# A two-layer decoder trunk on one core: hi and lo activations in one matmul of the feed-forward up-projection

## Chip, cores, metric

One core of one Trainium2 chip runs the whole program in one launch. The metric is device time in microseconds (us), the median of the timed runs. Five engines work in parallel, each through its own queue in program order: PE (TensorE, matmul), DVE (VectorE), ACT (ScalarE), POOL (GpSimd) and SP (SyncE, which here issues the loads).

## What is computed

x is 256 tokens of 1024 channels. Layer 0 has a sparse-attention mixer, layer 1 a state-space (SSD) mixer; each mixer is followed by a gated feed-forward with a causal convolution of width 3 along the tokens:

```python
def conv_ffn(h, w_up, conv_w, conv_b, w_down):
    u = causal_dwconv(h @ w_up, conv_w, conv_b)
    val, gate = u[..., :FFN_HIDDEN], u[..., FFN_HIDDEN:]
    return (jax.nn.silu(gate) * val) @ w_down
```

FFN_HIDDEN is 2816. The mixers take no part in the change.

## The kernel before, in words

**Products in three parts.** Every fp32 operand is split into a high part (a copy to fp32r by ACT) and a low part (source minus high, by DVE; `split`, L55 to L58). A product is then three matmuls: high by high, high by low, low by high (`mm3`, L166).

**Weights.** `Weights` (L71) loads a weight tile in halves of 128x1024 on SP's queue into `raw` (5 buffers), ACT casts the half to `whi` (L56), DVE makes `wlo` (L57), each from 5 buffers. A cast can start once PE is done with the buffer that it takes and the load has landed; the load can start once the `raw` buffer has been read.

**Feed-forward** (`ffn`, L536). The hidden channels are cut in 22 pairs p: 128 value channels (m=0) and the 128 gate channels that belong to them (m=1), each over all 256 tokens. Pairs 0 and 1 go through `proj_halves` (L183), while the second half of the tokens is still being normalised. Pairs 2 to 21 go through `pair` (L205): `proj_t` makes, for each m, 8 x 3 matmuls of 256 columns into one PSUM bank `pu` (two such banks are in turn). From `pu`, ACT makes the first tap of the convolution with the bias (`tap0`, L528), DVE the two other taps (`taps`, L534), ACT the gate's SiLU (L561), DVE the gate product (L562), and ACT and DVE split the result into the two parts of `hm`. The down-projection `down` takes `hm` of pair p-5 (LAG is 5): 12 matmuls of 512 columns into four banks `acc`. The last pairs' down-projections (5 in layer 0, 4 in layer 1; T0, T1) are left to the end, the first tokens' ahead of the second's; their weights have buffers of their own.

**What sets the order.** Each engine runs its queue as written. A conversion of weights stands in the queues of ACT and DVE where the recording layer put it, between the steps of the pairs, and whatever waits there holds what stands behind it. Before the feed-forward of layer 0 stands the attention; behind it the SSD mixer, whose first weights are loaded in the feed-forward's tail. Behind the feed-forward of layer 1 only the last normalisation and the store follow.

Of the kernel before, what the change touches and what calls it, by code (L numbers as in the profile page):

```python
# [7 lines left out]
F32 = mybir.dt.float32  # L8
F32R = mybir.dt.float32r
# [3 lines left out]
OP = mybir.AluOpType  # L13
AX = mybir.AxisListType

S, D = 256, 1024
KT = D // 128
FH = 2816
NP = FH // 128
# [14 lines left out]
def trunk(ctx, tc, x, gains, consts, masks, params, nsa_in, nsa_vw, cmp_w1, nsa_out,  # L34
          ssd_in, ssd_dt, ssd_out, ffn_up, ffn_down, out):
    nc = tc.nc
    cp = ctx.enter_context(tc.tile_pool(name="cp", bufs=1))
# [5 lines left out]
    def pa(shape, name):  # L43
        return pp.tile(shape, F32, name=name, tag="k" if name in ("pu", "pk", "pv", "po") else "t", bufs=2)

    def ps_(shape, name):
        return pp.tile(shape, F32, name=name, tag="s", bufs=4)
# [7 lines left out]
    def split(hi, lo, src, copy=nc.scalar.copy, eng=nc.vector):  # L55
        r = copy(hi, src)  # L56
        eng.tensor_tensor(lo, src, hi.bitcast(F32), op=OP.subtract)  # L57
        return r.ins  # L58

    def mm(*a, **k):  # L60
        last_mm[0] = nc.tensor.matmul(*a, **k)  # L61
        return last_mm[0]
# [30 lines left out]
    weights = Weights  # L93
# [33 lines left out]
        return rstd_of(ss[:, 0:1], ss[:, 1:2], 1)  # L127

    def new_xt():
        return (cp.tile([128, 2, KT, 128], F32R, name="xhi"), cp.tile([128, 2, KT, 128], F32R, name="xlo"))  # L130

    def after_ins(ins):
        return tc.issue_after(ins) if ins is not None else nullcontext()
# [37 lines left out]
    def proj_t(o, w, xt, c0, n=128):  # L171
        for k in range(KT):
            r = mm3(o, *w(k, slice(c0, c0 + n)), xt[0][:, :, k, :], xt[1][:, :, k, :], k == 0, k == KT - 1)
        return r.ins
# [8 lines left out]
    def proj_halves(ws, xt, pool, extra=None):  # L183
        marks = []
        u = [[pool.tile([128, 256], F32, name="ut", bufs=2 * len(ws)) for i in range(2)] for w in ws]
        for n, w in enumerate(ws):
            proj_half(w, xt, 0, u[n][0], marks)
        if extra:
            extra(0)
        pend(*marks[-FB:][:2])  # L190
        if extra:
            extra(1)
        for n in range(len(ws) + 1):
            if n < len(ws):
                proj_half(ws[n], xt, 1, u[n][1], marks)
            if n == 0:
                continue
            n -= 1
            ps = ps_([128, 2, S], "pu")
            for i in range(2):  # L200
                for m in range(2):
                    tr(ps[:, m, 128 * i:128 * i + 128], u[n][i][:, 128 * m:128 * m + 128], ident)
            yield ps

    def pair(w, xt, wide=False, order=[None]):  # L205
        ps = (ps_ if wide else pa)([128, 2, S], "pu")
        for m in range(2):
            order[0] = proj_t(ps[:, m, :], w, xt, 128 * m)
        return ps

    def out_mm(acc, i, jobs, first, last):
        marks = []
        ts = slice(128 * i, 128 * i + 128)
        for n, (a, ka, w, kw) in enumerate(jobs):
            for c in range(2):
                cs = slice(512 * c, 512 * c + 512)
                marks.append(mm3(acc[c], a[0][:, ka, ts], a[1][:, ka, ts], *w(kw, cs), first and n == 0,
                                 last and n == len(jobs) - 1).ins)
        return marks
# [307 lines left out]
    def tap0(c, ps, base, nt):  # L527
        nc.scalar.activation(c, ps, AF.Identity, bias=pr[:, base + nt:base + nt + 1],  # L528
                             scale=pr[:, base + nt - 1:base + nt])

    def taps(c, ps, base, nt):
        for s in range(1, nt):
            wv = pr[:, base + nt - 1 - s:base + nt - s]
            nc.vector.scalar_tensor_tensor(c[:, s:], ps[:, :S - s], wv, c[:, s:], op0=OP.mult, op1=OP.add)  # L534

    def ffn(l, fp, xt, after):  # L536
        lag, tail, nf = LAG, (T0, T1)[l], (N0, N1)[l]
        ex = max(tail, 2 * nf - 4)
        hs, wd = {}, {}
        first = proj_halves([weights(ffn_up[NP * l + p], KT, 256, *((fp, ex) if p >= 2 else ())) for p in range(nf)], xt, fp) if nf else None  # L540

        accs = []

        def down(ps, i):
            if not accs:
                accs.extend([ps_([128, 512], "acc") for c in range(2)] for i in range(2))
            return out_mm(accs[i], i, [(hs[p], 0, wd[p // 2], p % 2) for p in ps], ps[0] == 0, ps[-1] == NP - 1)

        for p in range(NP + lag):
            if p < NP:  # L550
                if p < nf:
                    ps = next(first)
                else:
                    ps = pair(weights(ffn_up[NP * l + p], KT, 256), xt)
                cc = fp.tile([128, 2, S], F32, name="cc", bufs=3)
                for m in (1, 0):
                    tap0(cc[:, m, :], ps[:, m, :], P_FC + 176 * l + 8 * p + 4 * m, 3)
                for m in (1, 0):
                    taps(cc[:, m, :], ps[:, m, :], P_FC + 176 * l + 8 * p + 4 * m, 3)
                    if m:  # L560
                        silu[0] = nc.scalar.activation(cc[:, 1, :], cc[:, 1, :], AF.Silu).ins  # L561
                nc.vector.tensor_tensor(cc[:, 0, :], cc[:, 0, :], cc[:, 1, :], op=OP.mult)  # L562
                hm = fp.tile([128, 2, 1, S], F32R, name="hm", bufs=tail + lag + 1)
                hs[p] = [hm[:, 0], hm[:, 1]]
                split(hm[:, 0, 0], hm[:, 1, 0], cc[:, 0, :])
            q = p - lag
            if q >= 0 and q % 2 == 0:
                late = q >= NP - tail
                wd[q // 2] = weights(ffn_down[(NP // 2) * l + q // 2], 2, D, *((fp, ex) if late else ()))
            if 0 <= q < NP - tail:  # L570
                for i in range(2):
                    down([q], i)
        marks = [down(range(NP - tail, NP), i) for i in range(2)][1]
        after(0, accs[0], marks[-FA:][:2])
        after(1, accs[1])


    def ssd(zp, yp, xt):
# [19 lines left out]
        def bc_unit(u, ps=None):  # L598
            if ps is None:
                ps = pair(weights(ssd_in[16 + u], KT, 256), xt, True)  # L600
            for m in range(2):
                t = 2 * u + m
                conv_tile(ps[:, m, :], 16 + t, bT[:, t, :] if t < 4 else cT[:, t - 4, :])
# [232 lines left out]


    xt = new_xt()
    gain0 = load_gain(0)
    scaled, *marks0 = prenorm(0, gain0, xt)  # L840
# [48 lines left out]
    for n, layer in enumerate((nsa, lambda *a: ffn(0, *a), ssd, lambda *a: ffn(1, *a))):  # L889
        nxt = new_xt() if n < 3 else None  # L890
        with tc.tile_pool(name=f"layer{n}", bufs=1) as pool:
            if n == 2:
                with tc.tile_pool(name="scan", bufs=1) as yp:
                    state = ssd(pool, yp, xt)
                with tc.tile_pool(name="ssd_out", bufs=1) as op_:
                    ssd_out_phase(op_, state, boundary(nxt))
            else:
                layer(pool, xt, boundary(nxt))
        xt = nxt
# [99 lines left out]
```

## Time and profile before

| | |
|---|---|
| runs | 740.83, 739.77, 740.40 us; median 740.4 |
| the profiled execution | 737.78 us, of which span 736.0 us |
| granted TensorE clock, mean | 0.993 |
| PE busy | 713.1 us (97%) |
| DVE busy | 567.2 us (77%) |
| ACT busy | 466.7 us (63%) |
| POOL busy | 75.8 us (10%) |

How to read it: the span is the profiled execution from its first to its last instruction; busy time is summed over the whole program, in which stages of different limits follow one another. A matmul's record is longer than its share of the engine, since matmuls overlap; what one costs in a stream is the stream's length over its count.

### The profile page before, as it was taken

Reading aid. Unit: us, or ns where it says so; the run is one execution under the profiler, and the core shown is the slowest. Engines: PE = TensorE matmul, PEld = TensorE weight load, DVE = VectorE, ACT = ScalarE, POOL = GpSimd, SP = SyncE. Lnnn points to the kernel's source line nnn. Section 1 sums busy time; section 2 is a strip of 40 time slices with the busy share of each in tenths; the row PEclk is TensorE's granted clock in tenths of the full one; section 3 lists DMA queues with packets and bytes.
Section 4 is the critical chain, followed back from the end, with each engine's and each line's share of the span. In section 5 each row is a group of like instructions: output and inputs, shape, how many; then the busy total and the mean of one; then the engine's idle time right before and its main releaser. Section 6 shows DMA issues by size and latency. Waiting matters only on the chain.

```text
span 736.0 us, 13745 instructions
## 1 busy us (share of the span) xinstructions
PE 713.1 (97%) x5252; PEld 658.0 (89%) x5252; DVE 567.2 (77%) x994; ACT 466.7 (63%) x879; POOL 75.8 (10%) x113
## 2 busy tenths in 40 slices
PE   7998999999999999999999999999989999999996
PEld 4998986779999999997999999998779999999995
DVE  4688898667867777688698878898888877767783
ACT  5577997447656555566776687765647655555551
POOL 2321442120000000001000000133120000000000
PEclk8999999999999999999999999999999999999998
DMA  8865431425655665564445574144655656555531
GB/s 313 297 220 181 140 119 59 142 79 185 199 197 173 193 202 182 195 218 154 139 166 172 181 232 133 58 139 148 200 172 172 200 175 200 197 185 189 181 106 57
DMA packets 35426, 126.07 MB, mean 171 GB/s; under 512 B 4065, under 2 KB 4385, under 8 KB 35361
## 3 DMA queue, kind: packets, MB, share of 16 engines
q1 hardware_dynamic: 35360, 125.20, 51.9%
q8 instruction: 41, 0.67, 0.4%
q14 instruction: 25, 0.20, 0.1%
HBM read 124.14 MB, written 1.05 MB: 170 GB/s over the span
## 4 chain that ended last, share of the span: by engine, by line
PE 77%; DVE 8%; ACT 7%; DMA 4%; issue 2%; POOL 1%; SPq 0%; DVEq 0%; POOLq 0%; ACTq 0%
PE pu L61 45%; PE acc L61 18%; PE pv L61 5%; DVE wlo L57 4%; ACT P L391 2%; PE pt L65 2%; ACT whi L56 2%; PE po L61 2%; ACT junk L126 1%; DMA raw<-in_nsa_in 1%; PE py L61 1%; DMA raw<-in_ffn_down 1%; DMA raw<-in_cmp_w 1%; DVE gw L799 1%; DMA raw<-in_ssd_out 1%
## 5 line engine op out<-in xcount | busy, mean ns | idle before, releaser
L57 DVE TENSOR_TENSOR wlo<-raw,whi 128x1024 fp32r<-128x1024 f32 (+1 forms) x219 | 270.5, 1240 | 79.9 <-ACT whi L56 79.2
L56 ACT CAST whi<-raw 128x1024 fp32r<-128x1024 f32 x223 | 230.8, 1045 | 111.0 <-PE pu L61 56.6
L61 PE MATMUL pu<-xhi,whi 128*128 128x256 f32 x1056 | 296.0, 281 | 1.5 <-DVE graw L288 1.5
L61 PE MATMUL pu<-xhi,wlo 128*128 128x256 f32 x1056 | 295.0, 280 | 1.5 <-DVE wlo L57 1.5
L61 PE MATMUL pu<-xlo,whi 128*128 128x256 f32 x1056 | 294.6, 279 | 0.0
L61 PEld LDWEIGHTS pu<-xhi,whi 128*128 128x128 f32 x1056 | 198.5, 188 | 3.4 <-ACT kd L358 1.6
L61 PEld LDWEIGHTS pu<-xhi,wlo 128*128 128x128 f32 x1056 | 198.4, 188 | 2.2 <-DVE wlo L57 2.1
L61 PEld LDWEIGHTS pu<-xlo,whi 128*128 128x128 f32 x1056 | 198.5, 188 | 1.2
L534 DVE SCALAR_TENSOR_TENSOR cc<-pu,pr,cc 128x255 f32<-128x255 f32 (+2 forms) x248 | 111.3, 477 | 6.7 <-ACT cc L528 3.6
L61 PE MATMUL acc<-whi,hm 128*128 128x512 f32 x352 | 114.6, 390 | 0.1
L61 PEld LDWEIGHTS acc<-whi,hm 128*128 128x128 f32 x352 | 66.1, 188 | 13.8 <-ACT hm L56 0.6
L61 PE MATMUL acc<-wlo,hm 128*128 128x512 f32 x176 | 68.9, 392 | 0.0
L528 ACT ACTIVATE cc<-pu,pr 128x256 f32<-128x256 f32 x112 | 57.8, 559 | 8.9 <-PE pu L61 8.8
L117 POOL TENSOR_SCALAR ms<-ss 128x1 f32<-128x1 f32 x16 | 7.9, 491 | 416.3 <-ACT junk L126 416.3
L56 ACT CAST hm<-cc 128x256 fp32r<-128x256 f32 x44 | 17.8, 404 | 44.9 <-DVE cc L562 44.9
L61 PE MATMUL acc<-whi,gw 128*128 128x512 f32 x128 | 41.3, 397 | 0.0
L61 PEld LDWEIGHTS acc<-wlo,hm 128*128 128x128 f32 x176 | 33.0, 188 | 5.6
L61 PE MATMUL pv<-whi,xhi 128*128 128x256 f32 (+1 forms) x128 | 36.8, 300 | 0.9 <-ACT xhi L56 0.4
L61 PE MATMUL pv<-whi,xlo 128*128 128x256 f32 (+1 forms) x128 | 35.5, 294 | 1.0 <-DVE xlo L57 0.9
L61 PE MATMUL pv<-wlo,xhi 128*128 128x256 f32 (+1 forms) x128 | 35.2, 285 | 0.2 <-DVE wlo L57 0.2
L391 ACT ACTIVATE P<-P,mx 128x128 f32<-128x128 f32 (+1 forms) x64 | 28.3, 447 | 2.9 <-DVE mx L389 2.9
L57 DVE TENSOR_TENSOR hm<-cc,hm 128x256 fp32r<-128x256 f32 x44 | 18.6, 424 | 14.6 <-ACT hm L56 14.6
(205 smaller groups left out, 862.7 us busy)
## 6 DMA issues: line engine op xcount, KB each, us to landing
raw<-in_ffn_up SPq DMA_DIRECT2D x88, 512.0 KB, 4.3
raw<-in_ffn_down SPq DMA_DIRECT2D x44, 512.0 KB, 4.6
raw<-in_ssd_in SPq DMA_DIRECT2D x40, 512.0 KB, 4.4
raw<-in_nsa_in SPq DMA_DIRECT2D x18, 512.0 KB, 5.1
raw<-in_ssd_out SPq DMA_DIRECT2D x16, 512.0 KB, 4.3
gain<-in_gains SPq DMA_DIRECT2D x8, 512.0 KB, 4.7
raw<-in_cmp_w SPq DMA_DIRECT2D x8, 512.0 KB, 6.3
raw<-in_nsa_out SPq DMA_DIRECT2D x8, 512.0 KB, 3.7
```

The source lines that it names most:

```text
L56: r = copy(hi, src)
L57: eng.tensor_tensor(lo, src, hi.bitcast(F32), op=OP.subtract)
L61: last_mm[0] = nc.tensor.matmul(*a, **k)
L65: last_mm[0] = nc.tensor.transpose(*a)
L117: nc.gpsimd.tensor_scalar(ms, a, b, EPS, op0=OP.mult if isinstance(b, float) else OP.add, op1=OP.add)
L126: nc.scalar.activation(junk, src[c], AF.Square, scale=1.0 / 32, accum_out=ss[:, c:c + 1])
L391: nc.scalar.activation(p, p, AF.Exp, scale=-1.0, bias=mx[:, qt, b:b + 1], accum_out=sums[:, qt, hh, b + 1:b + 2])
L528: nc.scalar.activation(c, ps, AF.Identity, bias=pr[:, base + nt:base + nt + 1], scale=pr[:, base + nt - 1:base + nt])
L534: nc.vector.scalar_tensor_tensor(c[:, s:], ps[:, :S - s], wv, c[:, s:], op0=OP.mult, op1=OP.add)
L799: nc.vector.scalar_tensor_tensor(gw[1][:, t, :], gg[:, t, :], nw, gw[0][:, t, :].bitcast(F32), op0=OP.mult, op1=OP.subtract)
```

## The change

Pairs 2 to 19 of each layer (36 in all) are made by a new `pair_wide`; pairs 0, 1, 20 and 21 stay as they are. The two parts of the activations now lie in one tile, so that one matmul of 512 columns multiplies a high weight by both parts; a second of 256 columns multiplies the low weight by the high part. A pair thus has 32 matmuls in place of 48, over the same 12288 columns. The gate half comes first and has a PSUM bank `pt`, the value half a bank `pv`. The two halves of a bank are then added into an SBUF tile `up`: ACT copies one, DVE adds the other; `tap0` and `taps` read `up`. The gate product of these pairs goes to POOL.

```diff
@@ -127,7 +127,8 @@
     def new_xt():
-        return (cp.tile([128, 2, KT, 128], F32R, name="xhi"), cp.tile([128, 2, KT, 128], F32R, name="xlo"))
+        both = cp.tile([128, 2, 2, KT, 128], F32R, name="xt")
+        return both[:, 0], both[:, 1], both.rearrange("p a b k t -> p (a b) k t")
@@ -207,6 +208,20 @@
+    def pair_wide(w, xt, dst):
+        for m in (1, 0):
+            ps = pa([128, 2, S], ("pv", "pt")[m])
+            cols = slice(128 * m, 128 * m + 128)
+            for k in range(KT):
+                hi, lo = w(k, cols)
+                if k:
+                    mm(ps[:, 0, :], lo, xt[0][:, :, k, :], start=False, stop=False)
+                mm(ps.rearrange("p a b -> p (a b)"), hi, xt[2][:, :, k, :], start=(k == 0), stop=(k == KT - 1))
+                if not k:
+                    mm(ps[:, 0, :], lo, xt[0][:, :, k, :], start=False, stop=False)
+            nc.scalar.copy(dst[:, m, :], ps[:, 1, :])
+            nc.vector.tensor_tensor(dst[:, m, :], ps[:, 0, :], dst[:, m, :], op=OP.add)
@@ -550,8 +565,11 @@
                 if p < nf:
                     ps = next(first)
+                elif p >= NP - 2:
+                    ps = pair(weights(ffn_up[NP * l + p], KT, 256), xt)
                 else:
-                    ps = pair(weights(ffn_up[NP * l + p], KT, 256), xt)
+                    ps = fp.tile([128, 2, S], F32, name="up", bufs=2)
+                    pair_wide(weights(ffn_up[NP * l + p], KT, 256), xt, ps)
@@ -559,7 +577,7 @@
-                nc.vector.tensor_tensor(cc[:, 0, :], cc[:, 0, :], cc[:, 1, :], op=OP.mult)
+                (nc.gpsimd if nf <= p < NP - 2 else nc.vector).tensor_tensor(cc[:, 0, :], cc[:, 0, :], cc[:, 1, :], op=OP.mult)
```

DVE's queue in the middle of layer 0's feed-forward, before the change: one pair from behind its predecessor's last step to its own (`cc` is the pair's convolution, `wlo` a converted weight half, `hm` the split result).

```order
L57 TENSOR_TENSOR wlo_3206<-raw_3203,whi_3205 128x1024
L57 TENSOR_TENSOR wlo_3212<-raw_3209,whi_3211 128x1024
L534 SCALAR_TENSOR_TENSOR cc_3106<-pu_3057,pr_126,cc_3106 128x255
L534 SCALAR_TENSOR_TENSOR cc_3106<-pu_3057,pr_126,cc_3106 128x254
L534 SCALAR_TENSOR_TENSOR cc_3106<-pu_3057,pr_126,cc_3106 128x255
L534 SCALAR_TENSOR_TENSOR cc_3106<-pu_3057,pr_126,cc_3106 128x254
L57 TENSOR_TENSOR wlo_3230<-raw_3227,whi_3229 128x1024
L562 TENSOR_TENSOR cc_3106<-cc_3106 128x256
L57 TENSOR_TENSOR hm_3115<-cc_3106,hm_3115 128x256
```

Two conversions stand ahead of the pair's taps, the third behind them, then the gate product and the low part of `hm`. The same stretch of DVE's queue after the change:

```order
L224 TENSOR_TENSOR up_2942<-pt_2955,up_2942 128x256
L549 SCALAR_TENSOR_TENSOR cc_2993<-up_2942,pr_125,cc_2993 128x255
L549 SCALAR_TENSOR_TENSOR cc_2993<-up_2942,pr_125,cc_2993 128x254
L57 TENSOR_TENSOR wlo_3083<-raw_3080,whi_3082 128x1024
L224 TENSOR_TENSOR up_2942<-pv_2974,up_2942 128x256
L57 TENSOR_TENSOR wlo_3089<-raw_3086,whi_3088 128x1024
L549 SCALAR_TENSOR_TENSOR cc_2993<-up_2942,pr_125,cc_2993 128x255
L549 SCALAR_TENSOR_TENSOR cc_2993<-up_2942,pr_125,cc_2993 128x254
L57 TENSOR_TENSOR wlo_3108<-raw_3105,whi_3107 128x1024
L57 TENSOR_TENSOR hm_3002<-cc_2993,hm_3002 128x256
```

Two adds are new, the conversions lie between the gate's and the value's steps, and the gate product is gone to POOL's queue, where it stands alone; the third conversion is right ahead of the low part of `hm`, which needs that product.

ACT's queue at the same place, before the change (`x2`: two in a row):

```order
L56 CAST whi_3023<-raw_3021 128x1024
L56 CAST whi_3029<-raw_3027 128x1024
L528 ACTIVATE cc_2924<-pu_2875,pr_126 128x256 x2
L56 CAST whi_3047<-raw_3045 128x1024
L561 ACTIVATE cc_2924<-cc_2924 128x256
L56 CAST hm_2933<-cc_2924 128x256
```

The casts of the weights run ahead of the steps that wait for DVE. After the change:

```order
L223 COPY up_2942<-pt_2955 128x256
L543 ACTIVATE cc_2993<-up_2942,pr_125 128x256
L56 CAST whi_3082<-raw_3080 128x1024
L579 ACTIVATE cc_2993<-cc_2993 128x256
L223 COPY up_2942<-pv_2974 128x256
L56 CAST whi_3088<-raw_3086 128x1024
L543 ACTIVATE cc_2993<-up_2942,pr_125 128x256
L56 CAST whi_3107<-raw_3105 128x1024
L56 CAST hm_3002<-cc_2993 128x256
```

Two copies are new, and the second and third cast now stand behind the gate's SiLU (L579), which waits for DVE's taps.

## Rows read from the trace of the kernel before

**Rows 1.** Chain that ended last: start, length (us), work; both feed-forwards.

```profile
173.56 22.17 PE pu L61 x190
195.73 2.75 PE acc L61 x12
198.48 5.60 PE pu L61 x48
...
312.51 1.06 ACT whi L56
...
327.56 3.87 DMA raw<-in_ssd_in
...
337.60 7.81 PE acc L61 x33
...
713.36 15.68 PE acc L61 x69
```

**Rows 2.** Windows: PE, PEld, DVE, ACT, POOL busy us (instructions), clock, DMA share, GB/s.

```profile
220.00:300.00 80.00, 80.00 (x573) 75.08 (x572) 59.10 (x88) 46.74 (x69) 0.00 (x0) 1.00 0.58 188
...
558.00:580.00 22.00, 22.00 (x189) 21.95 (x188) 20.49 (x37) 15.71 (x28) 0.00 (x0) 1.00 0.68 214
```

**Rows 3.** Groups by line and form, ACT, 160 to 340 us.

```profile
L56 ACT CAST whi<-raw 128x1024 fp32r<-128x1024 f32 x65 | 67.9, 1050 | 40.9 <-PE pu L61 20.3 <-PE acc L61 13.4 <-DMA raw<-in_ssd_in 3.0
L528 ACT ACTIVATE cc<-pu,pr 128x256 f32<-128x256 f32 x44 | 22.4, 559 | 0.0
L561 ACT ACTIVATE cc<-cc 128x256 f32<-128x256 f32 x22 | 9.1, 414 | 3.4 <-DVE cc L534 3.4
L56 ACT CAST hm<-cc 128x256 fp32r<-128x256 f32 x22 | 8.9, 404 | 21.4 <-DVE cc L562 21.4
L181 ACT COPY ut<-pv 128x256 f32<-128x256 f32 x4 | 1.5, 368 | 2.7 <-PE pv L61 2.7
L126 ACT ACTIVATE junk<-h 128x512 bf16<-128x512 f32 x2 | 1.3, 632 | 1.9 <-DVE h L164 1.9
L126 ACT ACTIVATE junk<-acc 128x512 bf16<-128x512 f32 x2 | 1.2, 597 | 1.1 <-PE acc L61 1.1
```

**Rows 4.** Groups by line and form, DVE, 160 to 340 us.

```profile
L57 DVE TENSOR_TENSOR wlo<-raw,whi 128x1024 fp32r<-128x1024 f32 x66 | 80.5, 1222 | 29.5 <-ACT whi L56 29.5
L534 DVE SCALAR_TENSOR_TENSOR cc<-pu,pr,cc 128x254 f32<-128x254 f32 x44 | 21.1, 481 | 1.4
L57 DVE TENSOR_TENSOR hm<-cc,hm 128x256 fp32r<-128x256 f32 x22 | 9.3, 424 | 7.1 <-ACT hm L56 7.1
L562 DVE TENSOR_TENSOR cc<-cc 128x256 f32<-128x256 f32 x22 | 9.2, 419 | 0.2
```

**Rows 5.** Timeline of DVE in layer 0's feed-forward: start us, length us.

```profile
255.16 1.23 DVE L57 TENSOR_TENSOR wlo<-raw,whi 128x1024 fp32r<-128x1024 f32 x1 [0.18 <-ACT whi L56]
256.31 1.90 DVE L534 SCALAR_TENSOR_TENSOR cc<-pu,pr,cc 128x255 f32<-128x255 f32 x4
258.12 1.22 DVE L57 TENSOR_TENSOR wlo<-raw,whi 128x1024 fp32r<-128x1024 f32 x1
...
262.11 1.23 DVE L57 TENSOR_TENSOR wlo<-raw,whi 128x1024 fp32r<-128x1024 f32 x1 [1.53 <-ACT whi L56]
```

**Rows 6.** Timeline of PE, the matmul that first reads that conversion.

```profile
266.73 0.28 PE L61 MATMUL pu<-xhi,wlo 128*128 128x256 f32 x1
```

**Rows 7.** Timeline of POOL in the SSD mixer's end.

```profile
490.76 1.60 POOL L803 TENSOR_TENSOR sq<-sq 128x256 f32<-128x256 f32 x1
...
495.81 0.81 POOL L803 TENSOR_TENSOR sq<-sq 128x256 f32<-128x256 f32 x1
```

**Rows 8.** Timeline of DVE at the same places.

```profile
490.22 1.54 DVE L57 TENSOR_TENSOR wlo<-raw,whi 128x1024 fp32r<-128x1024 f32 x1 [1.21 <-ACT whi L56]
...
495.94 1.76 DVE L57 TENSOR_TENSOR wlo<-raw,whi 128x1024 fp32r<-128x1024 f32 x1
```

**Rows 9.** Timeline of ACT in layer 0's feed-forward: casts of pair 18 and of pair 21.

```profile
309.79 0.41 ACT L56 CAST hm<-cc 128x256 fp32r<-128x256 f32 x1 [1.40 <-DVE cc L562]
...
337.14 0.41 ACT L56 CAST hm<-cc 128x256 fp32r<-128x256 f32 x1 [1.35 <-DVE cc L562]
```

**Rows 10.** Timeline of DVE, the last step of layer 1's pair 21.

```profile
717.37 0.43 DVE L57 TENSOR_TENSOR hm<-cc,hm 128x256 fp32r<-128x256 f32 x1 [0.47 <-ACT hm L56]
```

## The prediction

> **What bounds the kernel now.** I first read the chain that ended last [rows 1]. In both feed-forwards it lies on PE: 22.17 us for the opening pairs 2 to 5, which have no down-projection beside them yet, then for each pair 5.60 us of up-projection and 2.75 us of down-projection, a period of 8.35 us. In layer 0's tail, from 312.5 us, it leaves PE and runs through weight casts, conversions and loads until PE can go on at 337.6 us; in layer 1's tail it stays on PE. Second, the windows [rows 2]: from 220 to 300 us PE is busy 80.00 of 80 us at the full granted clock, DVE 59.1, ACT 46.7, POOL not at all. So in the steady part only PE's time counts, and the other engines have cover: DVE 2.2 us per period of 8.35. In the opening (558 to 580 us) the cover is thin: DVE is busy 20.49 of 22 us. The question is therefore what PE saves, and whether DVE, ACT and POOL, which now pass each pair between them more often, still fit in PE's period.
>
> **What PE saves.** A matmul of 256 columns takes 5.60/48 = 116.7 ns of the stream, one of 512 takes 2.75/12 = 229.1 ns [rows 1]. The change replaces two of the first by one of the second: 2 x 116.7 - 229.1 = 4.3 ns. With 16 merged per pair that is 0.07 us per pair, so PE's period becomes 8.28 us; 36 pairs give 2.5 us, half of it in each layer. If a merged matmul beside a short one does not cost as the down-projection's does, the gain lies between nothing (512 columns as dear as two times 256, 233.3 ns) and twice this (225 ns). I take the down-projection's 229.1, since it is the same operand type and width on the same engine. The Trainium skill, page "TensorE: Matmul & The Clock Gate", section "Back-to-back issue gap", gives N/2.4 + 2.5 ns for a lone matmul of N columns; by it a merge saves the 2.5 ns alone, 576 merges 1.4 us in place of my 2.5, and the trace's two cadences are both above the formula's 109.2 and 215.8 ns.
>
> **What the other engines get.** Per pair:
> - ACT: two copies of 128x256 out of PSUM, 0.37 us each [rows 3]; the first taps read SBUF in place of PSUM. The Square of 512 elements is 0.035 us longer from SBUF than from PSUM [rows 3], so I take 0.59 for the tap's 0.56. ACT goes from 4.9 us per period to 5.7, under the period.
> - DVE: two adds of 128x256, 0.42 each [rows 4]; the taps keep their 0.48, to be checked; the gate product, 0.42, goes. DVE's work grows from 6.2 to 6.6 us: by itself hidden.
> - POOL: one product of 128x256 of two SBUF operands. The nearest rows are the SSD mixer's: 0.81 us where nothing held it, 1.60 us where a DVE conversion ran when it started [rows 7]. That conversion ran from 490.22 to 491.76 and the POOL product ended at 492.36, 0.60 us behind it [rows 7, 8]. The other way round, a conversion of 1.22 us that met a POOL product took 1.76 us, ending 1.08 us behind it (495.94 to 497.70, product until 496.62). So these two do not run side by side; each waits out the other.
>
> **The loop.** More counts than the sum: DVE's queue now has the third conversion right ahead of the low part of hm, which needs POOL's product, and POOL can only end 0.60 us behind that conversion. I follow one pair when DVE's side is late and PE's results lie ready. Start at an hm cast. Handoffs are 0.03 us, instructions in a row on one engine follow each other about 0.09 us before the record's end (four taps take 1.90 us for 4 x 0.48; after 256.31 + 1.90 the next starts at 258.12 [rows 5]):
> hm cast and handoff 0.44; low part of hm on DVE 0.33 to the next; add of the gate half and handoff 0.45 (the copy beside it is ready); first tap 0.62; two taps 1.02; SiLU 0.32 and copy of the value half 0.27 on ACT; second weight cast 1.08; its conversion 1.14; the value's taps 0.90; third conversion 1.23; POOL's product 0.63 behind it. The sum is 8.43 us. (The first conversion and the value's add lie beside ACT's steps.)
> So the loop is 0.08 us longer than the old period and 0.15 longer than PE's new one. It does not hold at once: a conversion is done ahead of its use. The shortest such lead that I found is a second half of up weights, done at 262.11 + 1.23 = 263.34 and first read at 266.73 [rows 5, 6]: 3.4 us.
>
> **The sum.** Opening: five pairs (2 to 6) get two adds and lose a product, +0.42 x 5 = 2.1 us of DVE, against 1.5 us that were idle [rows 2]: at least +0.6 of lateness; the waits for POOL, about 1 us in each pair, could make it 3, but these pairs convert two halves and not three, which saves the loop 1.2. I take +1.0, near the low end. Then 12 periods to pair 18: 12 x 0.08 = +1.0. Its cast was at 309.79 us [rows 9], and would be 2.0 us later.
> Layer 0's tail has nothing to spare: its chain is conversions, loads and the last hm cast at 337.14 us [rows 9], whose result PE waits for at 337.6 [rows 1]. That cast is handed on from a chain that is 2.0 us late, so layer 0 ends 2.0 us later, and PE's gain there is lost. (Pairs 20 and 21 and their queue are as before.)
> Layer 1: by pair 19 DVE's side is 2.0 us later than before and PE 1.3 us earlier: 3.3 us, just under the 3.4 of the lead, so PE hardly stalls. In the tail the last hm was ready at 717.8 us [rows 10], while PE, starting its last row of matmuls at 713.36 [rows 1], comes to it some 40 matmuls of 0.229 us later, near 722.5: 4.7 us to spare, which takes up 3.3. Layer 1 keeps its -1.3.
> Sum: +2.0 - 1.3 = **+0.7 us**. Against the profiled execution, 737.8, that gives 738.5; it ran 2.6 us under the median, 740.4, so the forecast is 741.1. A run's median can tell about 0.2%, 1.5 us, from no change, so this is "no difference".
>
> The Trainium skill, page "GPSIMD Engine Reference", section "Engine selection", speaks against the move: it puts elementwise work on VectorE, GpSimd being about twice as slow with two inputs. Twice DVE's 0.42 would be an estimate of 0.84 by that page; the trace agrees with 0.81. By it the loop would grow 0.03 and the sum by some 0.4 us, to 741.5.
>
> **The rivals.**
> - *The cover holds in full.* If POOL's product runs beside the third conversion, it ends at 0.1 + 0.81 us behind the taps, before the conversion does; the loop is then 7.6 us, and if POOL wins the start and the conversion waits, 1.08 us behind it, about 8.1. Either is under 8.28: PE sets the pace in both layers, layer 0's tail starts earlier by PE's gain, and the time is 740.4 - 2.5 = 737.9. For it: the loop is only 0.15 us over, and a wait of 1.40 us ahead of ACT's hm cast [rows 9] is there today without harm. Against it: rows 7 and 8 show each waiting for the other. The page "SBUF — State Buffer" of the Trainium skill, section "SBUF: two separate sides", says the same as these rows, an exclusive lock for a DVE operation with two SBUF inputs against GpSimd.
> - *The loop becomes the bound* (ends on the other side). Place: POOL's product behind the third conversion. It decides from the point where the lateness exceeds the lead of 3.4 us before pair 19, that is at a loop of about 8.45. If POOL needs 0.75 to 0.91 us (its whole length and its start) behind the conversion instead of 0.60, the loop is 8.58 to 8.74. Layer 0 then ends 1.0 + 12 x 0.23 = 3.8 us later, or 5.7. Layer 1's lateness to PE is 1.0 + 13 x 0.30 = 4.9 or 7.0; beyond 3.4 PE stalls 1.5 or 3.6, less 1.3. In all +4.0 to +8.0; I name 745.5. For it: taps that now read two SBUF operands can also hold POOL back, and each conversion can slip behind its cast. Against it: one product of 0.81 in 8.3 us leaves POOL nothing else to do.
> - *The merge saves nothing*, 512 columns being as dear as two times 256: layer 1 gains nothing, layer 0 is as forecast, 740.4 + 2.0 = 742.4.
>
> **The numbers.** Forecast (the gain of layer 1 kept, layer 0's given back, 739.5 to 742.5): 0.42. Cover holds: 0.24. Loop bounds: 0.28. Nothing saved: 0.06. Faster by over 0.2% (under 738.9) is nearly all of the second, 0.24 with what the forecast's edge adds; slower (over 741.9) is the third, most of the fourth and the upper edge of the first, 0.38; the same 0.38. The range takes the second case and most of the third: 737.4 to 746.5.
>
> **What would show it.** Right: in the steady part up-projection pieces of 5.53 us; a period of 8.4 us between POOL's products, each ending about 0.6 us behind a conversion; the last hm cast of layer 0 some 2 us later than 337.14; PE unbroken in layer 1 and its last row earlier by about 1.3 us. Wrong: idle time of PE in the steady part released by conversions (loop bounds); products of 0.8 us beside conversions that keep 1.22 us (cover); a cadence of the merged matmul at 233 ns or under 226.

## The result and the profile after

The change made the kernel slower: 748.14 us median of 6 runs (747.29 to 749.99) against 740.36 us before; ratio 1.0108, 95% interval 1.0093 to 1.0122. The forecast was 741.1 us with a range up to 746.5, so the time lies 1.6 us above the range. It is the second rival that came true, the loop as the bound, which had a chance of 0.28. (Ratios and intervals are estimates from repeated runs and need not be the quotient of the two medians to the last digit.)

The chain that ended last, of the changed kernel: start, length in us, work. It answers to [rows 1].

```profile
176.56 2.44 PE pt L61 x14
...
263.43 1.57 POOL cc L580
...
269.64 1.23 DVE wlo L57
...
271.95 1.57 POOL cc L580
...
277.19 0.96 ACT whi L56
...
322.13 5.04 DMA raw<-in_ffn_down
...
334.23 5.51 DMA raw<-in_ssd_in
...
345.91 9.40 PE acc L61 x33
...
723.66 15.68 PE acc L61 x69
```

Before, the steady feed-forward lay on PE alone. Now the chain passes through POOL, DVE and ACT in every pair, once around per 8.53 us: POOL's products start at 263.43 and 271.95, and over the 13 periods from 212.23 to 323.19 us the mean is 8.535. PE's wait shows as small gaps in its own timeline, such as this one, where the low weights come late (the last column names the idle time and what ended it):

```profile
285.61 0.39 PE L61 MATMUL pt<-xt,whi 128*128 128x512 f32 x1
286.18 0.38 PE L61 MATMUL pt<-xt,wlo 128*128 128x256 f32 x1 [0.18 <-DVE wlo L57]
```

A matmul of 512 columns is followed by the next after 0.23 us elsewhere in this stream; here it is 0.57. Such gaps stand in every second pair, from 269.1 us on in layer 0 and from 659.9 us on in layer 1; they add up to about 1.3 us in each layer.

**Where the time went**, by starts in the chain. The span grew by 10.3 us in the profiled executions, the timed median by 7.8. Of the span's growth 3.0 us lie ahead of the first feed-forward, where the two programs are alike but for the layout of the activations: the last stretch of layer 0's pairs 0 and 1 starts at 170.41 us in place of 167.41. In the profiles of the kernels of this study, which are alike up to there in the same sense, that start lies anywhere from 167.4 to 170.5 us (one execution of 3976 us apart). I leave it out and measure each layer from such a common point:

| stretch | before | after | difference |
|---|---|---|---|
| layer 0, that start to the last down-projections | 170.19 | 175.50 | +5.31 |
| layer 0, these last down-projections (33 matmuls) | 7.81 | 9.40 | +1.59 |
| SSD mixer (the program is the same) | 205.10 | 204.92 | -0.18 |
| layer 1, the same start (550.51, 560.23) to the last down-projections | 162.85 | 163.43 | +0.58 |

These add up to +7.3 us, about what the timed medians differ by. Layer 0's part has a spread of its own. The chain of e11 below, which is the kernel before with another layout of the activations and takes the same time, has here:

```profile
328.95 5.56 DMA raw<-in_ssd_in
...
340.67 7.80 PE acc L61 x33
```

With its start at 169.09 us that is 171.58 us, 1.4 more than in the table, behind a load of 5.56 us in place of 3.87 [rows 1]. In e3 below, whose layer 0 is also the kernel before's, layer 0's down-projections end 0.2 us earlier than before. So of the +6.9 us of layer 0 some 5.5 to 7.1 are the change's.

The windows of the changed kernel around the end of layer 0 (columns as in [rows 2]) show what the 1.59 us are:

```profile
340.00:345.00 5.00, 1.12 (x5) 0.58 (x4) 4.02 (x7) 3.23 (x5) 0.00 (x0) 1.00 0.85 288
345.00:350.00 5.00, 4.09 (x11) 3.24 (x12) 2.02 (x5) 1.78 (x5) 0.34 (x2) 0.66 0.42 136
```

PE has nothing to do for nearly 5 us, waiting for the last hm; then it goes on at a granted clock of 0.66 on average over the second window, that is for part of the time at the lower of its two levels (1.2 and 2.4 GHz): from 346.42 to 349.41 us its matmuls start 0.43 us apart, later 0.23. The same 33 matmuls take 1.59 us longer. Before, PE was busy 4.87 of the 5 us from 337 to 342 and the clock stayed at 1.00.

**The loop itself.** One pair of the changed kernel on the three engines (start, length in us). DVE:

```profile
263.17 1.22 DVE L57 TENSOR_TENSOR wlo<-raw,whi 128x1024 fp32r<-128x1024 f32 x1
265.46 0.42 DVE L57 TENSOR_TENSOR hm<-cc,hm 128x256 fp32r<-128x256 f32 x1 [1.07 <-ACT hm L56]
265.80 0.42 DVE L224 TENSOR_TENSOR up<-pt,up 128x256 f32<-128x256 f32 x1
266.89 1.00 DVE L549 SCALAR_TENSOR_TENSOR cc<-up,pr,cc 128x255 f32<-128x255 f32 x2 [0.67 <-ACT cc L543]
267.83 1.23 DVE L57 TENSOR_TENSOR wlo<-raw,whi 128x1024 fp32r<-128x1024 f32 x1
268.98 0.42 DVE L224 TENSOR_TENSOR up<-pv,up 128x256 f32<-128x256 f32 x1
269.64 1.23 DVE L57 TENSOR_TENSOR wlo<-raw,whi 128x1024 fp32r<-128x1024 f32 x1 [0.25 <-ACT whi L56]
270.79 1.00 DVE L549 SCALAR_TENSOR_TENSOR cc<-up,pr,cc 128x255 f32<-128x255 f32 x2
271.70 1.22 DVE L57 TENSOR_TENSOR wlo<-raw,whi 128x1024 fp32r<-128x1024 f32 x1
```

ACT:

```profile
265.02 0.41 ACT L56 CAST hm<-cc 128x256 fp32r<-128x256 f32 x1 [2.49 <-POOL cc L580]
265.33 0.37 ACT L223 COPY up<-pt 128x256 f32<-128x256 f32 x1
266.25 0.60 ACT L543 ACTIVATE cc<-up,pr 128x256 f32<-128x256 f32 x1 [0.55 <-DVE up L224]
266.76 1.04 ACT L56 CAST whi<-raw 128x1024 fp32r<-128x1024 f32 x1
267.99 0.42 ACT L579 ACTIVATE cc<-cc 128x256 f32<-128x256 f32 x1 [0.19 <-DVE cc L549]
268.31 0.35 ACT L223 COPY up<-pv 128x256 f32<-128x256 f32 x1
268.57 1.05 ACT L56 CAST whi<-raw 128x1024 fp32r<-128x1024 f32 x1
```

POOL:

```profile
205.45 0.74 POOL L580 TENSOR_TENSOR cc<-cc 128x256 f32<-128x256 f32 x1 [5.79 <-DVE cc L549]
...
263.43 1.56 POOL L580 TENSOR_TENSOR cc<-cc 128x256 f32<-128x256 f32 x1 [6.97 <-DVE cc L549]
...
271.95 1.56 POOL L580 TENSOR_TENSOR cc<-cc 128x256 f32<-128x256 f32 x1 [6.97 <-DVE cc L549]
```

The reader is to see three things. POOL's product takes 1.56 us where it starts inside a conversion and 0.74 us where it does not; the conversion from 263.17 ends at 264.39 and the product at 264.99, 0.60 us behind it, as [rows 7, 8] gave it. DVE then stands idle 1.07 us ahead of the low part of hm and ACT 2.49 us ahead of its cast, both for POOL. And the gate's taps, the second conversion and the value's taps follow that cast one after the other, each waiting for the engine before.

### The profile page after: what moved, and what is told of

Read it like the earlier page. It is cut to its first block, busy times and chain, and to the rows that moved or that the text cites. A ratio compares the mean times of both kernels' runs of the same rounds, so it can differ in the third digit from the quotient of the medians.

```text
span 746.3 us, 12675 instructions
## 1 busy us (share of the span) xinstructions
PE 716.5 (96%) x4676; PEld 636.3 (85%) x4676; DVE 582.2 (78%) x1030; ACT 485.1 (65%) x951; POOL 130.0 (17%) x149
## 4 chain that ended last, share of the span: by engine, by line
PE 42%; DVE 25%; ACT 16%; POOL 7%; issue 5%; DMA 4%; POOLq 0%; SPq 0%; DVEq 0%; ACTq 0%
PE pu L61 17%; DVE wlo L57 10%; DVE cc L549 8%; PE acc L61 8%; PE pv L61 7%; POOL cc L580 6%; ACT whi L56 5%; PE pt L61 2%; ACT cc L543 2%; PE pt L65 2%; ACT P L406 2%; DVE hm L57 2%; DVE up L224 2%; ACT hm L56 2%; ACT cc L579 1%
## 5 line engine op out<-in xcount | busy, mean ns | idle before, releaser
L61 PE MATMUL pu<-xt,whi 128*128 128x256 f32 x960 | 172.7, 281 | 1.3 <-DVE graw L303 1.3
L61 PEld LDWEIGHTS pu<-xt,whi 128*128 128x128 f32 x960 | 146.9, 188 | 2.3 <-ACT kd L373 1.4
L61 PE MATMUL pu<-xt,wlo 128*128 128x256 f32 x480 | 134.7, 282 | 1.4 <-DVE wlo L57 1.4
L61 PE MATMUL pt<-xt,whi 128*128 128x512 f32 x288 | 104.2, 393 | 0.0
L61 PE MATMUL pv<-xt,whi 128*128 128x512 f32 x288 | 103.8, 393 | 0.0
L580 POOL TENSOR_TENSOR cc<-cc 128x256 f32<-128x256 f32 x36 | 54.7, 1519 | 260.3 <-DVE cc L549 222.7
L61 PEld LDWEIGHTS pu<-xt,wlo 128*128 128x128 f32 x480 | 90.2, 188 | 2.5 <-DVE wlo L57 2.2
L549 DVE SCALAR_TENSOR_TENSOR cc<-up,pr,cc 128x255 f32<-128x255 f32 (+1 forms) x144 | 71.9, 501 | 19.6 <-ACT cc L543 17.5
L61 PE MATMUL pt<-xt,wlo 128*128 128x256 f32 x288 | 76.2, 284 | 0.8 <-DVE wlo L57 0.8
L61 PE MATMUL pv<-xt,wlo 128*128 128x256 f32 x288 | 75.1, 281 | 0.0
```

Source lines behind the costliest of these rows:

```text
L580: (nc.gpsimd if nf <= p < NP - 2 else nc.vector).tensor_tensor(cc[:, 0, :], cc[:, 0, :], cc[:, 1, :], op=OP.mult)
```

## The experiments

**e1, the product back on DVE.**

```diff
-                (nc.gpsimd if nf <= p < NP - 2 else nc.vector).tensor_tensor(cc[:, 0, :], ...
+                nc.vector.tensor_tensor(cc[:, 0, :], ...
```

> The change with the gate product of pairs 2 to 19 back on VectorE; merged matmuls, copies and adds stay. Theory (the loop through POOL's product, 8.53 us per pair against PE's 8.31, makes the loss): without the 0.60 us behind the third conversion the loop is about 7.7 us, PE sets the pace again, layer 0's tail has no idle PE and no slow clock, and the time is before minus what merging saves (about 1.3 us): 739 us, 738.5 to 740.4. Rival one (the copies, adds and handoffs between engines are the loss, wherever the product is): over 744 us. Rival two (the lateness is one half, the tail's loads the other): about 743 us.

Measured: 738.14 us against 739.91 before on the same chip, ratio 0.9971 (0.9957 to 0.9986), 0.4 us under the range expected. The loss is gone once POOL's product alone is taken back, while the merged matmuls, the copies, the adds and all handoffs between PE, ACT and DVE stay: both rivals fall. The last down-projections take 7.82 us again. From the common starts layer 0 takes 0.41 us more than before, layer 1 0.80 us less. PE is never idle in the steady part of this kernel (windows, columns as in [rows 2]), though DVE is busier than in the change:

```profile
216.00:300.00 84.00, 84.00 (x445) 72.34 (x445) 70.31 (x111) 55.91 (x91) 0.00 (x0) 1.00 0.57 190
```

Its chain gives PE's pace, undisturbed:

```profile
206.09 2.72 PE acc L61 x12
208.81 2.79 PE pt L61 x16
211.60 2.79 PE pv L61 x16
...
305.77 2.72 PE acc L61 x12
```

Twelve periods from 206.09 to 305.77 us are 8.307 us each; before it was 8.345. That is 0.04 us per pair, or 2.4 ns for each of its 16 merged matmuls, in place of the 4.3 of the prediction. But the pieces show that most of it is not in the merged matmuls: the up-projection falls from 5.60 to 5.59 us (8.307 less 2.72), under 1 ns per merge, and the down-projection, whose matmuls were not changed, from 2.75 to 2.72. Why the latter runs faster here stays open.

**e2, POOL's product alone**, all pairs made as before:

```diff
-                elif p >= NP - 2:
+                elif p >= nf:
```

> The kernel before with nothing but the gate product of pairs 2 to 19 on POOL (three matmuls per k, taps from PSUM). Theory: POOL's product still ends 0.6 us behind a conversion, but two conversions now stand ahead of the taps in DVE's queue and none of the new handoffs is in the way, so a pair's loop is some 7 us, under PE's 8.35: 740.4 us, 739.5 to 742. Rival (DVE and POOL waiting for each other is the loss by itself, with or without the new handoffs): 744 to 748 us.

Measured: 738.88 us against 739.91, ratio 0.9990 (0.9982 to 0.9999). POOL's and DVE's timelines show the same wait as in the change:

```profile
267.14 1.50 POOL L580 TENSOR_TENSOR cc<-cc 128x256 f32<-128x256 f32 x1 [6.85 <-ACT cc L579]
269.11 0.43 DVE L57 TENSOR_TENSOR hm<-cc,hm 128x256 fp32r<-128x256 f32 x1 [1.07 <-ACT hm L56]
```

POOL's product is held up by the conversion here too, and DVE stands idle 1.07 us for it, without harm, since the loop around it is shorter than PE's period; that the product meets conversions is not enough for a loss. The steady part is as before: up-projection pieces of 5.60 us, down-projection 2.75. The expectation was a little too high, the rival is out.

**e3, the change in layer 1 alone.**

```diff
-                elif p >= NP - 2:
+                elif p >= NP - 2 or l == 0:
...
-                (nc.gpsimd if nf <= p < NP - 2 else nc.vector)
+                (nc.gpsimd if nf <= p < NP - 2 and l == 1 else nc.vector)
```

> The change in layer 1 alone; layer 0 is as before. Theory: layer 1 alone loses about 0.5 us (PE stalls of 1.2 us less 0.7 saved), because its tail has time to spare; nearly all of the loss is layer 0's tail: 740.9 us, 740 to 741.8. Rival (each layer loses alike, half of 7.8 us): 744.3 us.

Measured: 740.81 us against 739.91, ratio 1.0010 (0.9991 to 1.0029). From its start (553.23 us) to its last down-projections (716.69) layer 1 takes 163.46 us, 0.61 more than before and as in the full change. That is as the theory had it; the layers don't lose alike.

**e5, pairs 16 to 21 as before.**

```diff
-                elif p >= NP - 2:
+                elif p >= NP - 6:
...
-                (nc.gpsimd if nf <= p < NP - 2 else nc.vector)
+                (nc.gpsimd if nf <= p < NP - 6 else nc.vector)
```

> The change for pairs 2 to 15 alone; pairs 16 to 21 are made as before, with the product on VectorE. Theory (lateness carried into layer 0's tail makes the loss): the four narrow pairs take up about 1.4 us of lateness each, what there was at pair 15 (about 3 us) is gone before the tail, no idle PE, no slow clock: 739.5 us, 739 to 741. Rival (the tail is long for a reason of its own, such as its loads or the slow clock, whatever the lateness): 743 to 746 us.

Measured: 739.73 us against 739.91, ratio 0.9998 (0.9988 to 1.0007). Fourteen wide pairs per layer with their POOL products cost nothing if four pairs with a shorter loop follow: the last down-projections of layer 0 start 170.94 us behind the common start (175.50 in the change) and take 7.79 us. Counted from that start, the cast of hm is 2.9 us later than before at pair 15 and 0.1 us earlier at pair 18, so the narrow pairs took the lateness up, at first by about 1.3 us each. In layer 0 the lateness thus does its harm where it meets the tail. PE's wait ahead of the last down-projections is 1.4 us from start to start, in place of 5.2 in the change, and the clock stays up: the slow clock comes of the long wait.

**e6, the whole end of a pair on POOL.**

```diff
-                split(hm[:, 0, 0], hm[:, 1, 0], cc[:, 0, :])
+                split(hm[:, 0, 0], hm[:, 1, 0], cc[:, 0, :], *((nc.gpsimd.tensor_copy, nc.gpsimd) if nf <= p < NP - 2 else ()))
```

> The change with the whole end of a pair on POOL: product, cast and low part of hm of pairs 2 to 19, so that nothing in DVE's or ACT's queue waits for POOL. POOL and DVE still hold each other up, now with three POOL operations per pair. Theory (the loss is that the queues of DVE and ACT wait for POOL's product): the loop of DVE and ACT falls to about 7.2 us plus at most 1 us of waits for POOL, PE sets the pace: 738.5 to 741 us. Rival (the mutual waiting of DVE and POOL is itself the loss): with three POOL operations it grows, 748 us or more.

Measured: 738.77 us against 740.29, ratio 0.9985 (0.9973 to 0.9998). One pair of this kernel on POOL's timeline:

```profile
268.54 1.82 POOL L580 TENSOR_TENSOR cc<-cc 128x256 f32<-128x256 f32 x1 [5.20 <-ACT whi L56]
270.43 0.40 POOL L56 CAST hm<-cc 128x256 fp32r<-128x256 f32 x1
270.91 0.74 POOL L57 TENSOR_TENSOR hm<-cc,hm 128x256 fp32r<-128x256 f32 x1
```

The product is held up still longer than in the change (1.82 us against 1.56) and POOL is twice as busy, yet the loss is gone, since no instruction in DVE's or ACT's queue waits for it any more. DVE and ACT also have some 0.4 us less work each per pair here, but e1, where DVE has more work than in the change, shows that the loss does not hang on that. What cost the time was thus not the mutual waiting as such but where it stood: on the loop between a conversion and the next pair's first steps, in the queues of both other engines.

**e9, the product made twice.**

```diff
+                if nf <= p < NP - 2:
+                    dup = fp.tile([128, S], F32, name="dup", bufs=1)
+                    nc.gpsimd.tensor_tensor(dup, cc[:, 0, :], cc[:, 1, :], op=OP.mult)
                 (nc.gpsimd if nf <= p < NP - 2 else nc.vector).tensor_tensor(...
```

> The change with POOL's product made twice, once into a tile that nobody reads. Theory (POOL's product lies on the loop that sets the pace in both layers): the loop grows by about 0.75 us to 9.28, layer 0 by 12 to 13 of these, layer 1 by 13, with all of its time: 748.1 + 19 = 767 us, 764 to 770. Rival (the loop is set by DVE's and ACT's steps, and the product fits beside them): under 752 us.

Measured: 775.24 us against 740.29, ratio 1.0472 (1.0459 to 1.0486), that is 27 us more than the change. The way was foreseen, the size was not: 19 was expected. On POOL's timeline the first product waits out the conversion, the second follows:

```profile
233.32 1.58 POOL L582 TENSOR_TENSOR dup<-cc 128x256 f32<-128x256 f32 x1 [6.94 <-DVE cc L549]
234.99 0.74 POOL L583 TENSOR_TENSOR cc<-cc 128x256 f32<-128x256 f32 x1
...
242.66 1.59 POOL L582 TENSOR_TENSOR dup<-cc 128x256 f32<-128x256 f32 x1 [6.94 <-DVE cc L549]
```

The loop is 9.34 us, 0.81 longer (0.74 and the step from one to the next). Against the change layer 0 grew by 13.2 us up to its last down-projections, layer 1 by 13.3: some 16 times 0.81, not 12 to 13 times. The opening pairs, which I had left out of the count, are on the loop too: by pair 6 the cast of hm is already 3.5 us later than in the change.

**e7, short matmuls behind the long ones**, to see what makes the merged matmul dear; the product is on DVE:

```diff
             for k in range(KT):
-                hi, lo = w(k, cols)
...
+                mm(ps.rearrange("p a b -> p (a b)"), w(k, cols)[0], xt[2][:, :, k, :], start=(k == 0), stop=False)
+            for k in range(KT):
+                mm(ps[:, 0, :], w(k, cols)[1], xt[0][:, :, k, :], start=False, stop=(k == KT - 1))
```

> As e1_product_on_dve, but in each half of a pair the eight matmuls of 512 columns run in a row, then the eight of 256, in place of in turns. Theory (a matmul of 512 columns in turns with one of 256 costs 232.6 ns, in a row 229): a half takes 2.77 us in place of 2.79, 1.9 us less in all, about 736 us. Rival (the merged matmul costs 232 to 233 ns in any order): a half stays at 2.79 us, the time at e1's 738.1 within 0.7.

Measured: 741.34 us against 740.29, ratio 1.0014 (1.0004 to 1.0025). PE's timeline of one half:

```profile
262.73 2.03 PE L61 MATMUL pv<-xt,whi 128*128 128x512 f32 x8
264.60 1.10 PE L61 MATMUL pv<-xt,wlo 128*128 128x256 f32 x8
265.53 0.40 PE L61 MATMUL acc<-whi,hm 128*128 128x512 f32 x1
```

From start to start the eight long ones take 1.87 us, 234 ns each, the short ones 116 ns. The order is not what makes the merged matmul dear; in turns it is even a little cheaper (in e1's trace 231 ns from its start to the next, the short one 118). The down-projection and a whole period are longer here too, 2.78 and 8.40 us, and with them the time. The theory falls; the rival was near with the price, but expected e1's time.

**e10, one stretch in place of four pieces**, on e1:

```diff
-        both = cp.tile([128, 2, 2, KT, 128], F32R, name="xt")
-        return both[:, 0], both[:, 1], both.rearrange("p a b k t -> p (a b) k t")
+        both = cp.tile([128, KT, 2, 2, 128], F32R, name="xt")
+        hi, lo = [both[:, :, a].rearrange("p k i t -> p i k t") for a in range(2)]
+        return hi, lo, both.rearrange("p k a i t -> p (a i) k t")
```

> As e1_product_on_dve, with the tile of the activations laid out so that the 512 columns of a merged matmul (and the 256 of a short one) lie in one stretch, in place of four (two) pieces of 128. Theory (the merged matmul's 233 ns, against 229 for the down-projection's, come from reading four pieces): a half of a pair falls from 2.79 to about 2.75 us or less, 36 pairs give 2.3 us or more against e1: 735.9 us, 734 to 736.5. Rival (the pieces cost nothing; the merged matmul costs 233 ns for another reason): a half stays at 2.79, the time within 0.7 us of e1's 738.1.

Measured: 738.8 us, the median of eleven executions between 737.1 and 742.3, against 740.42, ratio 0.9983 (0.9968 to 0.9999). The execution that was profiled took 3976 us, so no trace gives the length of a half here. By the time there is no gain over e1 of the 2.3 us foreseen.

**e11, the same layout in the kernel before**, with the product on DVE:

> The kernel before with that layout of the activations alone (three matmuls of 256 columns per k, product on DVE). Theory (pieces cost): a matmul of 256 columns falls below 116.7 ns, by 1 to 2 ns, 48 x 36 and more of them give 2 to 4 us: 736 to 738.5 us. Rival: 116.7 ns as before, 740.2 us within 0.7.

Measured: 740.2 us against 740.42, ratio 0.9995 (0.9982 to 1.0009). Up-projection pieces stay at 5.60 us for 48 matmuls. The layout does not set the 116.7 ns; for the merged matmul only the time of e10 speaks. Why the merged matmul takes longer than the down-projection's stays open.

**e8, wide pairs to the end**, on e1 (pairs 20 and 21 too):

```diff
-                elif p >= NP - 2:
+                elif p >= NP:
```

> As e1_product_on_dve, with pairs 20 and 21 made by wide matmuls too. Theory (layer 0's tail has no time to spare on DVE, so each add there counts; PE saves 0.04 us per pair): 0.5 to 1 us above e1, 738.6 to 739.2 us. Rival (the tail is set by its loads): as e1 or 0.15 us less, 738.0.

Measured: 738.74 us against 740.29, ratio 0.9980 (0.9969 to 0.9990). Beside e1's 0.9971 that is the same; it doesn't tell the two expectations apart. From the common start layer 0's last down-projections begin at 170.48 us, with e1 at 170.60.

## Why the prediction was wrong

**What bounds the kernel.** Right: PE set the pace, and the question was whether the loop fits in PE's period. The loss began where the second rival had put it, at POOL's product behind the third conversion. The forecast chose the wrong side of a threshold that it had set itself at a loop of about 8.45 us. Its own sign of this, PE waiting in the steady part for a conversion, stands in the line at 286.18 above.

**The loop: the first step that failed.** The forecast had 8.43 us, the trace has 8.53. By the rows above, from the hm cast at 265.02 to the next at 273.55, with the forecast's term in brackets: cast 0.44 (0.44), low part 0.34 (0.33), add 0.45 (0.45), first tap 0.64 (0.62), gate's taps up to the SiLU 1.10 (1.02), SiLU 0.32 (0.32), copy 0.26 (0.27), weight cast 1.07 (1.08), conversion 1.15 (1.14), value's taps 0.91 (0.90), third conversion and POOL's product 1.81 (1.83), handoff 0.04 (0.03). POOL's 0.60 us was right; 0.08 of the 0.10 us that were missing lie in the gate's taps and the handoff behind them, as the chain shows:

```profile
266.89 0.50 DVE cc L549
...
267.41 0.49 DVE cc L549
...
267.93 0.02 ACTq L579
267.94 0.04 issue
267.99 0.42 ACT cc L579
```

The second tap starts 0.52 us behind the first and the SiLU 0.09 behind the second's end, of which 0.06 pass in ACT's sequencer and behind it; the forecast's handoff was 0.03. I had put the whole uncertainty of the loop on POOL, and POOL's term was the one that came out as estimated. So PE was late where it was to be "unbroken": see layer 1.

**PE's gain.** Mis-sized too: 0.04 us per pair and not 0.07, so PE's period became 8.31 and not 8.28. I had set the down-projection's 229.1 ns for the merged matmul, and it takes 231 to 234. By the pieces of e1 the merge itself gave under 1 ns of the 4.3, close to the fourth rival (the merge saves nothing); the rest of the 0.04 us lies in the down-projection. The page "TensorE: Matmul & The Clock Gate" of the Trainium skill, section "Back-to-back issue gap", gives 2.5 ns per merge by its formula, an estimate. The trace does not bear it out: e1's period alone gives 2.4 ns, but its pieces show under 1 ns in the merged stream, and all cadences lie above the formula.

**Layer 0: the tail, the second step that failed.** The forecast had +2.0; it is +6.9. By its own rule, lateness at pair 18 is 1.0 + 12 x (8.535 - 8.345) = 3.3 us; measured from the common start that cast is 3.5 us late (316.25 against 309.79, less 3.0). The opening's +1.0 was thus about right (1.2 at pair 6). But the tail added to what it was handed, where the forecast said that it hands the lateness on as it is. The load of the down weights in its chain is issued 4.3 us late (322.13 against 314.84, less 3.0), since the conversion that frees its buffer now stands behind the gate's steps; some 0.6 us of that are made up in the tail, and the next load of the chain takes 5.51 us in place of 3.87 [rows 1]. Together that is the +5.3. The longer load also occurs in kernels that lose nothing (5.53 us in e1, 5.37 in e2, 5.56 in e11), so it is not caused by the lateness; up to 1.4 us of the +5.3 may be that the profiled execution of the kernel before was a quick one. Why the load varies was not tried. The last 1.6 us, the slow clock behind an idle PE, were put at nothing in the forecast; e9, where PE waits as long there, loses them too (10.49 us for the 33 matmuls).

**Layer 1.** The forecast had -1.3: the lateness, 3.3 us, just under the lead of 3.4. With 8.53 and 8.31 it is 1.0 + 13 x 0.225 = 3.9 us, above the lead, and PE stalls, by that rule 0.5 us. Without the product on POOL the layer gains 0.80 us, with it it loses 0.6: the stalls cost 1.4. So the lead was also taken too large. PE first waits at 269.1 us in layer 0, some 6.5 turns behind pair 6, when the rule gives a lateness of 2.5 us (an estimate: 1.0 + 6.5 x 0.228). That the tail of layer 1 takes up the rest was right.

**Both steps were needed.** With a loop of 8.53 and PE's 8.31 the forecast's own rules give +3.3 for layer 0 and -0.2 for layer 1, 743.5 us, still in the range. What took the time out of it is what the rules lacked: the tail of layer 0 (+1.8 over the lateness handed on, and 1.6 of slow clock) and the shorter lead of layer 1.

**The rivals.** "The loop becomes the bound" came true, with +7.3 us by the trace in its span of +4.0 to +8.0. That the span holds it is in part luck: its condition, that POOL needs 0.75 us or more behind the conversion, did not occur, and by its rules a loop of 8.53 gives some +3 us. The range was cut at 746.5 inside that span, little more than half of it, though the point of decision, 8.45, lay only 0.02 us above the forecast's loop, which does not bear out a chance as low as 0.28. "The cover holds" has the time that e1 and e6 show once the wait is out of the queues (738.1 and 738.8 for its 737.9), but not by its mechanism: POOL and DVE still wait for each other in e6. The warning of the page "GPSIMD Engine Reference" of the Trainium skill, section "Engine selection", held as a rule (0.74 us on POOL alone, 0.42 on DVE), but the length of the operation alone decided nothing: e2 moved the same product without loss.

**Better than both kernels** is e1: the merged matmuls with the product on DVE, 0.29% (0.14 to 0.43) under the kernel before. Its profile accounts for 0.4 us of the 1.8 in the two feed-forwards against the kernel before, and for all 1.8 against e11; how much is the merge's is not settled, since layer 0's tail varies by 1.6 us, and the part ahead of the feed-forwards by up to 3 us, from execution to execution.

## What to carry to other kernels

When work moves to another engine, don't compare busy times; follow one item around all queues and add up the steps that wait for each other, then compare that loop with the bound engine's period. A loop that comes out within 2% of the period is a coin's toss, and the range must reach as far as the losing side goes: 0.2 us per turn became 7 us with a tail that had no room and a clock that fell while PE waited. An operation that can be held up does no harm if nothing in a busy queue waits behind it (e6), or if the loop that waits for it is shorter than the period (e2).

## What the runs showed of the hardware

- A matmul of 512 fp32r columns with the activations as the moving side took 231 ns in turns with short ones and 234 in a row, against 227 to 232 (2.72 to 2.78 us for 12) in the down-projection; two of 256 take 233.4. Merging gave under 1 ns a piece in the merged stream itself.
- A POOL product of 128x256 took 0.74 us when alone, 1.56 us when it began inside a DVE conversion, ending 0.60 us behind it, in one period after the other.
- After nearly 5 us without work PE went on at a granted clock of 0.66 in the window from 345 to 350 us, and 33 matmuls took 9.40 us in place of 7.81; after a gap of 1.4 us (e5) they took 7.79.
